# The up projection of the second batch as seven products of half blocks, with sums of blocks kept on chip

## The chip, the cores and the metric

The kernel runs on one core of one Trainium2 chip. The metric is device time in microseconds for one execution. Both request batches (1024 tokens each) go through the same layer within that one execution.

## What the kernel must compute

The reference is a hybrid encoder layer. What matters here is its feed-forward part, which each batch passes after the attention half:

```python
def _conv_ffn(x, l, prm):
    h = x @ prm['ffn_up'][l]                     # (1024, 1024) @ (1024, 5632)
    cw = prm['conv_w'][l]
    h = cw[0] * _shift_prev(h) + cw[1] * h + cw[2] * _shift_next(h) + prm['conv_b'][l]
    gate, up = jnp.split(h, 2, axis=-1)
    return (jax.nn.gelu(gate, approximate=False) * up) @ prm['ffn_down'][l]

x = _layer_norm(ALPHA * x + mixed, ...)
x = _layer_norm(ALPHA * x + _conv_ffn(x, l, prm), ...)
```

## The kernel before

All dense products are made in a split form: every float32 operand is written as a high part (`hi`, rounded to float32r by a ScalarE copy) and a low part (`lo`, the rest), and a product is three matmuls, hi·hi, hi·lo and lo·hi. The activations lie transposed in SBUF as `self.xT` = (`xh`, `xl`), each [128, 8 blocks of the model dimension, 1024 tokens]. Weights come from DRAM as 128 x 1024 blocks (`weights`, L229) or pairs of 128 x 512 (`load` in `dense_t`, L274), and are split by ScalarE (`hi`, L248) and GpSimd (`lo`, L251).

The feed-forward part has two stages for each batch. `phase_f1` (L1057) is the up projection. Its loop over j runs over 22 blocks of 128 gate columns; for each j it takes the gate block m = j and the up block m = 22 + j. Each m is one [128, 1024] tile of PSUM (`dpsum`, tag `d`, two buffers of two banks each) filled by `dense` (L253): two halves of 512 tokens, 8 blocks of the model dimension, three matmuls each, so 48 matmuls. Then ScalarE and VectorE do the width-3 convolution out of PSUM (L1070, L1071, L1073), GELU and the gating product (L1076, L1077), and the hidden block is split into hi and lo (`hilo`, L304). `phase_f2` (L1085) is the down projection, for four 128-token tiles at a time (j = 0, 1), over two halves of the output columns (n = 0, 1) and 22 blocks k.

The second batch's two stages are the last ones of the kernel, with nothing else left to interleave. There the hidden blocks of the first 512 tokens stay in SBUF (`keep`, 22 blocks of [128, 2, 512]); those of the other 512 tokens are stored to DRAM as they are made and loaded back during the second stage, into the space of `xh` and `xl`.

Two things order the work. The program is written with tiles and tags: tiles of one tag share a fixed number of buffers (`BUFS`: seven of `t`, four of `w`, two of `whi`; four PSUM banks for the two-buffer tag `d`, four for `spsum`'s tags `a` and `b`). And a planner lays out each engine's instruction order when the program is built, by priority (the order of the code) and by its own estimate of when each instruction is ready:

```python
with tile.TileContext(nc, schedule_with_timeline_sim=True) as tc, ExitStack() as ctx:
```

On the chip each engine runs its list in that order and waits on semaphores. All loads and stores named here are issued by SyncE (line 79, `ld`).

## Time and profile before

| | |
|---|---|
| median of 3 runs | 3606.48 us (3603.18 to 3615.9) |
| the profiled execution's own time | 3613.08 us |
| its span in the trace | 3611.3 us |
| mean granted TensorE clock | 0.944 |
| TensorE matmul busy | 3254.0 us, 90% of the span |
| up projection of the second batch, from the turn to full rate to its last matmul | about 2866 to 3345 us |
| down projection of the second batch and end | 3345 to 3611 us |

The lines of a trace give the kernel's line, the engine (PE is TensorE's matmuls, PEld its weight loads, DVE VectorE, ACT ScalarE, POOL GpSimd, SP SyncE; a q behind the name is the engine's queue), the operation, the tiles written and read, their shapes, and times in microseconds unless marked ns. A matmul's duration overlaps that of the next one, so the rate is read from a count over a stretch of time. PEclk is the granted clock of TensorE as a share of its full 2.4 GHz.

### The profile page before, as it was taken

How to read it: one execution, taken by the hardware profiler on the slowest of the kernel's cores; microseconds unless marked ns; L12 is line 12 of the kernel's file. 1: busy time of each engine (PE TensorE's matmuls, PEld its weight loads, DVE VectorE, ACT ScalarE, POOL GpSimd, SP SyncE). 2: the span in 40 equal slices, each digit the busy share in tenths (PEclk: the TensorE clock that was granted, in tenths of full speed). 3: DMA queues.
4: the chain of work that ended last, by engine and by line, in shares of the span. 5: the costliest groups of instructions: out<-in, count | busy, mean ns of one | idle time of the engine just before them, and what ended most of it. 6: DMA issues, size and time to landing. Idle time of an engine off the chain costs nothing. (4 is left out here: it accounts for less than half of the span.)

```text
span 3611.3 us, 56096 instructions
## 1 busy us (share of the span) xinstructions
PE 3254.0 (90%) x21477; PEld 2584.8 (72%) x21477; DVE 1961.5 (54%) x3550; ACT 1379.4 (38%) x2349; POOL 1292.2 (36%) x1387
## 2 busy tenths in 40 slices
PE   5788888998999986789999999989987899999997
PEld 4566666676777874567777787767865688888876
DVE  6378873335557866888534445366685633333022
ACT  3233332443245643345334343334454422332222
POOL 5365441001422445544121112363352622222464
PEclk9898888998999998788999999999999999999999
DMA  5568774534455655567543336586552322222642
GB/s 161 163 201 228 211 193 126 154 106 118 128 171 155 215 200 165 162 153 166 127 133 115 117 104 210 175 261 209 185 188 93 114 71 71 70 70 70 225 172 87
DMA packets 603360, 545.59 MB, mean 151 GB/s; under 512 B 205341, under 2 KB 477965, under 8 KB 603093
## 3 DMA queue, kind: packets, MB, share of 16 engines
q1 hardware_dynamic: 536532, 508.44, 46.3%
q10 hardware_dynamic: 66560, 33.56, 3.9%
q8 instruction: 171, 2.80, 0.3%
q14 instruction: 97, 0.79, 0.1%
HBM read 361.49 MB, written 180.39 MB: 150 GB/s over the span
## 5 line engine op out<-in xcount | busy, mean ns | idle before, releaser
L251 POOL TENSOR_TENSOR w<-w,whi 128x256 fp32r<-128x256 f32 (+1 forms) x800 | 758.6, 975 | 1246.1 <-ACT whi L248 1088.0
L264 PE MATMUL d<-xh,whi 128*128 128x512 f32 (+1 forms) x2112 | 863.7, 409 | 17.8 <-DVE t L399 6.0
L265 PE MATMUL d<-xl,whi 128*128 128x512 f32 (+1 forms) x2112 | 855.2, 405 | 0.6 <-DVE xl L308 0.6
L266 PE MATMUL d<-xh,w 128*128 128x512 f32 (+1 forms) x2112 | 853.7, 404 | 2.1 <-POOL w L251 2.1
L248 ACT ACTIVATE whi<-w 128x512 fp32r<-128x512 f32 (+1 forms) x536 | 307.9, 622 | 728.7 <-PE d L290 234.5
L264 PEld LDWEIGHTS d<-xh,whi 128*128 128x128 f32 (+1 forms) x2112 | 408.7, 194 | 117.3 <-issue 8.8
L266 PEld LDWEIGHTS d<-xh,w 128*128 128x128 f32 (+1 forms) x2112 | 407.9, 193 | 99.7 <-POOL w L251 3.3
L265 PEld LDWEIGHTS d<-xl,whi 128*128 128x128 f32 (+1 forms) x2112 | 408.2, 193 | 93.5 <-issue 2.0
L1071 DVE SCALAR_TENSOR_TENSOR t<-d,cols,t 128x1023 f32<-128x1023 f32 x88 | 112.8, 1282 | 455.7 <-ACT t L1070 442.6
L288 PE MATMUL d<-whi,xh 128*128 128x512 f32 x640 | 259.2, 413 | 31.5 <-DVE t L1051 15.1
L289 PE MATMUL d<-w,xh 128*128 128x512 f32 x640 | 259.2, 405 | 0.9 <-POOL w L251 0.9
L290 PE MATMUL d<-whi,xl 128*128 128x512 f32 x608 | 245.7, 404 | 0.0
L1051 DVE SCALAR_TENSOR_TENSOR t<-t,d 128x512 f32<-128x512 f32 x112 | 72.7, 678 | 244.7 <-PE d L290 240.7
L928 ACT ACTIVATE e<-e,ms 128x1024 f32<-128x1024 f32 x128 | 147.1, 1149 | 123.8 <-DVE ms L926 105.3
L935 POOL TENSOR_SCALAR e<-e,ms 128x512 f32<-128x512 f32 x128 | 88.1, 701 | 268.8 <-DVE ms L933 110.7
L288 PEld LDWEIGHTS d<-whi,xh 128*128 128x128 f32 x640 | 123.9, 194 | 66.7 <-DVE rs L1051 11.9
L739 DVE TENSOR_TENSOR G<-s,ms 64x256 f32<-64x256 f32 x128 | 53.4, 417 | 171.4 <-PE s L724 170.3
L289 PEld LDWEIGHTS d<-w,xh 128*128 128x128 f32 x640 | 124.0, 194 | 29.5 <-POOL w L251 2.2
L290 PEld LDWEIGHTS d<-whi,xl 128*128 128x128 f32 x608 | 117.2, 193 | 28.3 <-issue 1.0
L919 PE MATMUL s<-k,qh 128*128 128x512 f32 x256 | 113.9, 446 | 25.9 <-DVE ms L922 15.6
L619 DVE TENSOR_TENSOR Ntmp<-N 128x30 f32<-128x30 f32 (+14 forms) x240 | 111.3, 464 | 34.0 <-DMA N<-abd 29.0
L758 POOL COPY vr<-v 128x256 f32<-128x256 f32 x32 | 13.0, 405 | 324.4 <-DMA v<-va 311.3
(228 smaller groups left out, 5944.9 us busy)
## 6 DMA issues: line engine op xcount, KB each, us to landing
w<-in_ffn_up SPq DMA_DIRECT2D x88, 512.0 KB
w<-in_ffn_down SPq DMA_DIRECT2D x88, 512.0 KB
h<-t SPq DMA_DIRECT2D x66, 512.0 KB
ab<-AB ACTq DMA_DIRECT2D x64, 512.0 KB
w<-in_w_in SPq DMA_DIRECT2D x58, 512.0 KB
G<-ab SPq DMA_DIRECT2D x128, 128.0 KB
BK<-ab SPq DMA_DIRECT2D x64, 256.0 KB
w<-in_w_out SPq DMA_DIRECT2D x32, 512.0 KB
```

The costliest lines, as they stand in the source:

```text
L248: nc.scalar.activation(out=hi[:, s], in_=w[:, s], func=AF.Copy)
L251: nc.gpsimd.tensor_tensor(out=lo[:, s], in0=w[:, s], in1=hi[:, s].bitcast(F32), op=ALU.subtract)
L264: nc.tensor.matmul(o, wh, rh, start=first, stop=False)
L265: nc.tensor.matmul(o, wh, rl, start=False, stop=False)
L266: nc.tensor.matmul(o, wl, rh, start=False, stop=last)
L288: nc.tensor.matmul(out[i], lh, wh, start=k == ks[0], stop=False)
L289: nc.tensor.matmul(out[i], lh, wl, start=False, stop=False)
L290: nc.tensor.matmul(out[i], ll, wh, start=False, stop=k == ks[-1])
L619: nc.vector.tensor_tensor(out=tv, in0=N[:, 0:j, j : j + 1].to_broadcast([P, j, w]), in1=N[:, j : j + 1, j + 1 : 32].to_broadcast([P, j, w] ...
L919: nc.tensor.matmul(pp, q_[0], k_[c][:, ks], start=True, stop=False)
L928: nc.scalar.activation(out=e_, in_=e_, func=AF.Exp, bias=ms[:, 2 + c : 3 + c], accum_out=ms[:, 4 + c : 5 + c])
L1071: nc.vector.scalar_tensor_tensor(out=o[:, 1:T], in0=pp[:, 0 : T - 1], scalar=self.cw[0][:, m : m + 1], in1=o[:, 1:T], op0=ALU.mult, op1=AL ...
```

## The change

In the second batch, and there only, the up projection for j = 2 to 21 is no longer made by `dense`. The pair of weight blocks (gate and up, 256 columns by 1024) and the activations (1024 by 1024 tokens) are each seen as 2 x 2 blocks, and their product is made by seven half-block products (12 matmuls each) in place of eight, by the scheme of Winograd: sums S1 to S4 of weight blocks are formed for each j by VectorE and split anew; sums T1 to T4 of activation blocks are formed once, at j = 2, by `right`, of which T1, T2 and T4 have tiles of their own and T3 is written over the activation block b12 in `xh` and `xl`. Partial sums that enter more than one result are passed on inside PSUM by ScalarE copies between matmul groups, and one product (`e`) is added by VectorE. The space of `keep` is now taken by T, S and the split sums (`o`), so all hidden blocks go to DRAM, and the down projection loads all of them back, into the space of the seven right-hand blocks (28 slots, in the order in which `seven` uses them). `pre` is now called in both halves n; in the attention output stage it does nothing for n = 1. The first batch keeps its path.

```diff
-    def phase_f1(self, b, keep=None):
+    def phase_f1(self, b, tl=None):
...
         for j in range(KF):
             gu = []
-            for m in (j, KF + j):
-                ws = self.weights(I["ffn_up"][0], m * P, KT)
-                pp = self.dpsum()
-                self.dense(pp, ws, rhs, (0, 1), KT)
+            if tl and j == 2:
+                right = self.right(tl)
+            pps = self.seven(tl, j, right) if tl and j >= 2 else None
+            for i, m in enumerate((j, KF + j)):
+                pp = pps[i] if pps else eight(m)
...
             for half in range(2):
-                stay = keep is not None and half == 0
-                o = keep[:, j] if stay else self.dt("t", F32R, shape=(P, 2, 512))
+                o = self.dt("t", F32R, shape=(P, 2, 512))
                 self.hilo(gu[1][:, 512 * half : 512 * half + 512], o[:, 0], o[:, 1])
-                if not stay:
-                    self.ld(out=S["h"][j][half], in_=o)
...
+                self.ld(out=S["h"][j][half], in_=o)
+        return right[:7] if tl else None
+
+    def right(self, tl):
+        nc = self.nc
+        xh, xl = self.xT
+        block = lambda a, b: [tuple(x[:, 4 * a + k, 512 * b : 512 * b + 512] for x in (xh, xl)) for k in range(4)]
+        T = [tl(f"T{i}", dt=F32R, shape=(P, 4, 2, 512)) for i in (1, 2, 4)]
+        op = lambda out, a, b, o: nc.vector.tensor_tensor(out=out, in0=a, in1=b, op=o)
+        two = lambda: self.dt("t", shape=(P, 2, 512))
+        for q in range(2):
+            b11, b12, b21, b22 = ([x[:, 4 * a + 2 * q : 4 * a + 2 * q + 2, 512 * b : 512 * b + 512].bitcast(F32)
+                                   for x in (xh, xl)] for a in range(2) for b in range(2))
+            at = [t[:, 2 * q : 2 * q + 2] for t in T]
+            t1, u = two(), two()
+            op(t1, b12[0], b11[0], ALU.subtract)
+            nc.gpsimd.tensor_tensor(out=u, in0=b12[1], in1=b11[1], op=ALU.subtract)
+            op(t1, t1, u, ALU.add)
+            self.hilo(t1, at[0][:, :, 0], at[0][:, :, 1])
+            op(t1, b22[0], t1, ALU.subtract)
+            op(t1, t1, b22[1], ALU.add)
+            self.hilo(t1, at[1][:, :, 0], at[1][:, :, 1])
+            op(t1, b21[0], t1, ALU.subtract)
+            op(t1, t1, b21[1], ALU.add)
+            self.hilo(t1, at[2][:, :, 0], at[2][:, :, 1])
+            t3, u = two(), two()
+            op(t3, b22[0], b12[0], ALU.subtract)
+            nc.gpsimd.tensor_tensor(out=u, in0=b22[1], in1=b12[1], op=ALU.subtract)
+            op(t3, t3, u, ALU.add)
+            self.hilo(t3, *(x[:, 2 * q : 2 * q + 2, 512:1024] for x in (xh, xl)))
+        of = lambda t: [(t[:, k, 0], t[:, k, 1]) for k in range(4)]
+        return [of(T[0]), block(0, 0), of(T[1]), block(1, 0), block(0, 1), block(1, 1), of(T[2])]
+
+    def seven(self, tl, j, right):
+        nc, w = self.nc, self.I["ffn_up"][0]
+        raw = []
+        for m in (j, KF + j):
+            raw.append(self.dt("w", shape=(P, 8, P)))
+            self.ld(out=raw[-1], in_=w[:, m * P : (m + 1) * P].rearrange("(k p) c -> p k c", p=P))
+        a11, a12, a21, a22 = (r[:, 4 * h : 4 * h + 4] for r in raw for h in range(2))
+        op = lambda out, a, b, o: nc.vector.tensor_tensor(out=out, in0=a, in1=b, op=o)
+        s1, s2, s3, s4 = (tl("S", 4, shape=(P, 4, P)) for _ in range(4))
+        op(s1, a21, a22, ALU.add)
+        op(s2, s1, a11, ALU.subtract)
+        op(s4, a12, s2, ALU.subtract)
+        op(s3, a11, a21, ALU.subtract)
+        ha, la = self.dt("whi", F32R, shape=(P, 8, P)), self.dt("w", F32R, shape=(P, 8, P))
+        left = {}
+        for name, a in (("s1", s1), ("a11", a11), ("s2", s2), ("a12", a12), ("s3", s3), ("s4", s4), ("a22", a22)):
+            if name in ("a11", "a12"):
+                hi, lo = (x[:, 0:4] if name == "a11" else x[:, 4:8] for x in (ha, la))
+            else:
+                hi, lo = (tl("o", 16, F32R, (P, 4, P)) for _ in range(2))
+            nc.scalar.activation(out=hi, in_=a, func=AF.Copy)
+            nc.gpsimd.tensor_tensor(out=lo, in0=a, in1=hi.bitcast(F32), op=ALU.subtract)
+            left[name] = hi, lo
+
+        def product(o, a, b, first):
+            (ah, al), b = left[a], right[b]
+            for k in range(4):
+                for x, (l, r) in enumerate(((ah, 0), (ah, 1), (al, 0))):
+                    nc.tensor.matmul(o, l[:, k], b[k][r], start=first and k == x == 0, stop=k == 3 and x == 2,
+                                     skip_group_check=True)
+
+        e, p1, p2 = self.spsum(), self.dpsum(), self.dpsum()
+        c11, c12, c21, c22 = (p[:, 512 * h : 512 * h + 512] for p in (p1, p2) for h in range(2))
+        product(e, "s1", 0, True)
+        product(c11, "a11", 1, True)
+        nc.scalar.copy(out=c12, in_=c11)
+        product(c12, "s2", 2, False)
+        nc.scalar.copy(out=c21, in_=c12)
+        product(c11, "a12", 3, False)
+        product(c21, "s3", 4, False)
+        es = self.dt("t")[:, 0:512]
+        nc.scalar.copy(out=es, in_=e)
+        op(c22, c21, es, ALU.add)
+        product(c12, "s4", 5, False)
+        op(c12, c12, es, ALU.add)
+        product(c21, "a22", 6, False)
+        return p1, p2
...
-    def phase_f2(self, b, out, keep=None):
+    def phase_f2(self, b, out, slots=None):
...
-                parts = [(range(KF), {k: keep[:, k] if j == 0 else slots[k] if k < 16 else keep[:, k - 16] for k in range(KF)})]
+                at = {(jj, k): slots[(KF * jj + k) % len(slots)] for jj in range(2) for k in range(KF)}
+                parts = [(range(KF), {k: at[j, k] for k in range(KF)})]
+
+            def fill(jj, k):
+                for x in range(2):
+                    self.ld(out=at[jj, k][x], in_=S["h"][k][jj][:, x])
...
-                    if keep is None or j == 1 and k >= 16:
-                        self.ld(out=at[k], in_=S["h"][k][j])
-                    elif j == 0 and 4 <= k < 20:
-                        self.ld(out=slots[k - 4], in_=S["h"][k - 4][1])
+                    if slots is None:
+                        if n == 0:
+                            self.ld(out=here[k], in_=S["h"][k][j])
+                    elif j == 0 and n == 0:
+                        for kk in range(4) if k == 0 else ():
+                            fill(0, kk)
+                        if k + 4 < KF:
+                            fill(0, k + 4)
+                    elif j == 0:
+                        fill(1, k)
...
         with self.tc.tile_pool(name="f1", bufs=1) as pool:
-            h = pool.tile([P, KF, 2, 512], F32R, name="h")
-            self.phase_f1(1, h)
-            self.phase_f2(1, y1, h)
+            def tl(tag, bufs=1, dt=F32, shape=(P, 512)):
+                return pool.tile(list(shape), dt, name=self.nm(tag), tag=tag, bufs=bufs)
+
+            right = self.phase_f1(1, tl)
+            self.phase_f2(1, y1, [at for block in right for at in block])
```

## Rows read from the trace of the kernel before

**Rows 1.** the page, busy time of each engine over the span

```profile
PE 3254.0 (90%) x21477; PEld 2584.8 (72%) x21477; DVE 1961.5 (54%) x3550; ACT 1379.4 (38%) x2349; POOL 1292.2 (36%) x1387
```

**Rows 2.** stages: length, busy us (instructions) by engine, PEclk, DMA share, GB/s

```profile
2905.00:3000.00 95.00, 95.00 (x409) 76.96 (x408) 30.78 (x29) 29.04 (x39) 24.14 (x35) 1.00 0.23 75
...
3345.00:3365.00 20.00, 19.16 (x83) 15.19 (x82) 5.08 (x5) 5.71 (x9) 7.59 (x6) 1.00 0.95 361
3365.00:3465.00 100.00, 99.89 (x441) 82.36 (x440) 3.68 (x6) 21.91 (x38) 48.09 (x38) 1.00 0.45 154
```

**Rows 3.** groups of 2905 to 3345 us: shapes xcount, busy us, mean ns, idle

```profile
L264 PE MATMUL d<-xh,whi 128*128 128x512 f32 x629 | 249.9, 397 | 0.0
...
L251 POOL TENSOR_TENSOR w<-w,whi 128x256 fp32r<-128x256 f32 x152 | 108.0, 742 | 317.6 <-ACT whi L248 317.6
...
L1071 DVE SCALAR_TENSOR_TENSOR t<-d,cols,t 128x1023 f32<-128x1023 f32 x39 | 50.0, 1283 | 270.3 <-ACT t L1070 270.3
L1070 ACT ACTIVATE t<-d,cols 128x1024 f32<-128x1024 f32 x39 | 46.5, 1192 | 0.0
L248 ACT ACTIVATE whi<-w 128x512 fp32r<-128x512 f32 x78 | 45.0, 624 | 175.3 <-PE d L265 92.8 <-issue 77.0 <-PE d L266 5.4
L1077 DVE TENSOR_TENSOR t<-t,t 128x1024 f32<-128x1024 f32 x19 | 23.3, 1226 | 0.7
L1076 ACT ACTIVATE t<-t 128x1024 f32<-128x1024 f32 x20 | 21.2, 1062 | 54.6 <-DVE t L1073 54.6
L308 DVE TENSOR_TENSOR t<-t,t 128x512 fp32r<-128x512 f32 x20 | 13.7, 685 | 0.0
...
L307 ACT ACTIVATE h<-t 128x512 fp32r<-128x512 f32 x19 | 12.0, 632 | 74.7 <-DVE t L1077 74.7
```

**Rows 4.** duration ns min/median/max of single lines

```profile
L1051 DVE SCALAR_TENSOR_TENSOR t<-t,d x24: 670/681/689, 2794.1 to 3594.4; 128x512 f32<-128x512 f32 x24
...
L307 ACT ACTIVATE xh<-s x16: 572/582/600, 2813.5 to 2860.0; 128x512 fp32r<-128x512 f32 x16
```

**Rows 5.** the group of L251 at 512 columns, 3365 to 3590 us

```profile
L251 POOL TENSOR_TENSOR w<-w,whi 128x512 fp32r<-128x512 f32 x80 | 101.5, 1290 | 102.3 <-ACT whi L248 102.3
```

**Rows 6.** SyncE in order of time, one load pair of the first stage

```profile
2998.05 11.57 SPq L79 DMA_DIRECT2D w<-in_ffn_up  x2
```

**Rows 7.** SyncE's waits, 2860 to 3600 us: total, times, longest

```profile
SPq L79 <- PE d L266: 297.7, 46, 11.5
```

**Rows 8.** SyncE in order of time at the second stage's start

```profile
3345.25 0.38 SPq L79 DMA_DIRECT2D w<-in_ffn_down  x1
3345.68 0.94 SPq L79 DMA_DIRECT2D xh<-h  x2
3346.67 2.77 SPq L79 DMA_DIRECT2D t<-x  x4
```

**Rows 9.** the turn between the stages in order of time

```profile
3345.02 0.40 PE L288 MATMUL d<-whi,h 128*128 128x512 f32 x1
...
3348.64 1.28 DVE L1073 SCALAR_TENSOR_TENSOR t<-d,cols,t 128x1023 f32<-128x1023 f32 x1
...
3349.81 0.39 PE L288 MATMUL d<-whi,h 128*128 128x512 f32 x1
...
3351.75 0.62 ACT L307 ACTIVATE t<-t 128x512 fp32r<-128x512 f32 x1
```

**Rows 10.** the turn into the first stage, in 20 us windows

```profile
2820.00:2840.00 20.00, 17.10 (x82) 12.82 (x81) 19.25 (x33) 8.26 (x14) 14.77 (x13) 1.00 0.38 131
2840.00:2860.00 20.00, 15.35 (x76) 11.67 (x74) 15.56 (x21) 9.12 (x16) 16.88 (x16) 0.91 0.36 132
2860.00:2880.00 20.00, 19.37 (x72) 15.51 (x73) 4.07 (x5) 7.41 (x9) 5.72 (x8) 0.84 0.19 53
```

**Rows 11.** TensorE in order of time after the gap

```profile
2865.06 0.63 PE L264 MATMUL d<-xh,whi 128*128 128x512 f32 x1
```

**Rows 12.** line L334 on VectorE, beside GpSimd's half: ns min/median/max

```profile
L334 DVE TENSOR_TENSOR t<-t,t x44: 675/1205/1865, 8.5 to 3604.7; 128x512 f32<-128x512 f32 x44
```

More of the change, by code (lines that the diff above doesn't have):

```diff
@@ L1053, in residual @@
         for n in range(2):
-            self.dense_t(w, 512 * n, ks, lhs, range(4 * g, 4 * g + 4), put, n, pre if n == 0 else None, last and n == 1)
-    def phase_f1(self, b, keep=None):
+            self.dense_t(w, 512 * n, ks, lhs, range(4 * g, 4 * g + 4), put, n, lambda k: pre(k, n), last and n == 1)
+    def phase_f1(self, b, tl=None):
         nc, I, S = self.nc, self.I, self.st[b]
@@ L1086, in phase_f2 @@
+    def phase_f2(self, b, out, slots=None):
         nc, I, S = self.nc, self.I, self.st[b]
         gb = []
-        slots = [x[:, k0 + k].rearrange("p (a t) -> p a t", a=2) for k0 in (0, 4) for x in self.xT for k in range(4)]
+        own = [x[:, k0 + k].rearrange("p (a t) -> p a t", a=2) for k0 in (0, 4) for x in self.xT for k in range(4)]
         for j in range(2):
@@ L1091, in phase_f2 @@
             rs = {}
[L1092 to L1093 removed]
+            if slots is None:
+                parts = [(range(k0, min(k0 + 8, KF)), {k: own[8 * ((3 * j + k0 // 8) % 2) + k % 8] for k in range(k0, min(k0 + 8, KF))})
                          for k0 in range(0, KF, 8)]
             else:
[L1096 removed]
```

23 lines of the change are left out of this document (15 added, 8 removed).

## The prediction

> **What bounds the kernel now.** I read the page first: TensorE is busy for 3254.0 us, VectorE for 1961.5, ScalarE and GpSimd for less than 1400 each [rows 1]. A whole-kernel share proves nothing for one stage, so the second view is the one by windows. In the up projection of the second batch TensorE is busy 95.00 us of 95.00 at a granted clock of 1.00, while VectorE, ScalarE and GpSimd stand at 24 to 31 us of those 95 [rows 2]. The third view, by line, gives the rate: the groups of L264, L265 and L266 have 629 matmuls each in the 440 us from 2905 to 3345, with no idle time in front of them [rows 3], so one matmul takes 440 / 1887 = 0.2332 us. This stage is TensorE throughput and nothing else; work taken off TensorE here is worth its full price as long as no wait appears in its place. The down projection behind it is the same: 99.89 us busy of 100 [rows 2]. The chain that ended last runs through these matmuls in both stages, so I costed the change on TensorE's list and asked of every other engine only whether TensorE will wait for it.
>
> **What is removed.** A pair of blocks cost 2 x 48 = 96 matmuls and costs 7 x 12 = 84 now. For 20 pairs that is 240 matmuls fewer: 240 x 0.2332 = **56.0 us**, the ceiling of the gain. One new pair is 84 x 0.2332 = 19.6 us of TensorE.
>
> **What is added on other engines, per pair.** VectorE: four convolution passes of 1.283, the gating product 1.226, two low parts of 0.685 [rows 3], the four sums S at the nearest price, that of a low part (0.685), two additions out of PSUM at 0.68, the row of L1051 [rows 4]: 5.13 + 1.23 + 1.37 + 2.74 + 1.36 = 11.8 us. ScalarE: two convolution passes 1.192, GELU 1.062, two high parts 0.632, seven splits 0.624 [rows 3], three copies out of PSUM at 0.582, the row that reads PSUM [rows 4]: 10.8 us. GpSimd: seven subtractions at 1.290 [rows 5] = 9.0 us. All are below 19.6, so none becomes the bound by throughput. The weights have a lead: 16 buffers of `o` hold a pair and a half, so they are split about a pair ahead. These additions cost nothing while that cover lasts.
>
> **Waits that are new, per pair.** Before, a PSUM tile had a whole block's time (48 x 0.2332 = 11.2 us) to be emptied. Now two waits stand on TensorE's list. First, a11 must be copied from c11 to c12 before s2 adds to it: no other product of the pair is free then (a12 adds to c11, which is being copied). That is one copy, 0.582, plus the drain of the last matmul (its 0.397 duration less the 0.233 rate [rows 3]) and whatever ScalarE has in hand: I take 1.0 to 1.3 us. The second copy (c12 to c21) lies under a12, 2.8 us. Second, p1 is final only after s4 and the addition of e, and must be read out before the next pair's a11: 0.68 + 1.192 + 2 x 1.283 = 4.4 us [rows 3, 4], of which a22 covers 12 x 0.2332 = 2.8. The rest, 1.6 plus queueing behind one operation in flight, about 2.3, can be covered by the next pair's s1, which goes into `e` and needs neither p1 nor p2. p2 has three further products as cover and costs nothing. The planner does fill such gaps with later products: at the turn into the down projection TensorE goes on without a break from 3345.02 to 3349.81 while the second PSUM tile is still being read by L1073 [rows 9]. But one s1 (2.8 us) has to fill two gaps that sum to 3.3 to 3.6. Bounds: 0.2 us per pair if the filling works out, 2.9 if each gap stays open once. I take 0.9, close to the filled case because of [rows 9]: 20 x 0.9 = **18 us**.
>
> **The sums of activations, once.** `right` has 24 VectorE passes over 1024 columns at 1.226 [rows 3], 29.4 us, and eight high parts and four GpSimd subtractions beside them. Whether TensorE waits depends on when they may start. Their inputs are ready before the stage begins, and VectorE is two thirds idle there. But they need `t` buffers, and buffers of a tag seem to be given in the order of the code. The load of the next weight block waits for the last matmul that reads a low part (297.7 us in 46 waits) [rows 6, 7], although a raw block's buffer was free much earlier, when GpSimd finished its split; that free one is held for the low part that precedes the load in the code. Likewise the four `t` loads of the down projection, coded ahead of the two `xh` loads, are issued behind them [rows 8]. By that order the sums start when the pair j = 1 gives its last `t` tile, 6.7 us after its last matmul (3345.02 to 3351.75 for the last pair [rows 9]), and VectorE ends them 29.4 us later at the earliest. a22 for T4 stands at the end: 6.7 + 29.4 + half of a22, 1.4, = 37.5 us from j = 1 to the end of j = 2, where 19.6 are due: 18 us lost, less 2.8 if s1 of j = 3 fills in. The gap also lowers the clock: ahead of this stage TensorE was busy for 15.35 of 20 us, and in the next 20 us the granted clock averaged 0.84, a matmul showing 0.63 us in place of 0.40 [rows 10, 11], which is 0.16 x 20 = 3 us. Bounds: 2 (sums done early, only T3's split, which must wait for j = 1's reads, in the way; a12 and three other products cover it) and 21. I take **15**.
>
> **The turn and the down projection.** At the end no s1 is left as cover, so p1's and p2's read-out shows: 2 us (0 to 5). The hidden blocks of the first 512 tokens now come from DRAM: 768 KB per block k in 2.8 us is 281 GB/s. Before, 16 of the 22 blocks had the same load (other halves fetched ahead), at 361 GB/s with TensorE busy 19.16 of 20 us [rows 2]. The slots come free in the order of the last pair's products, from its s1 on, some 17 us before they are read. SyncE's queue has more, shorter issues (0.47 us each [rows 8]): 61 in 61 us, half its time. I take 2 us (0 to 8). For the stores, doubled, the DMA engines have room at 75 GB/s [rows 2]. The attention output stage and the first batch issue the same instructions as before.
>
> **Sum.** -56.0 + 18 + 15 + 2 + 2 = **-19 us**. From the profiled execution's 3613.08 that is 3594; it stood 6.6 above the median of the runs shown, so against 3606.48 I predict **3587.5 us**. Its own range: 3576 to 3599.
>
> **The rivals.** (1) *The sums start early*: buffers are given as they come free and `right` runs under j = 0 and 1. The idle VectorE speaks for it, [rows 6 to 8] against. Entry 2 in place of 15: 3574.5, down to 3562 with 0.3 us per pair. (2) *The gaps stay open*: the copy and part of p1's read-out cost TensorE 1.85 us per pair; 20 x 1.85 = 37, with the 19 elsewhere, gives the whole gain back: 3606. For it: the plan is laid out from estimates, and a list that is off by 0.5 us in two places cannot be reordered. (3) *VectorE and GpSimd block each other, slower*: a VectorE sum of two SBUF tiles of 512 columns takes 0.685 in this stage [rows 3] but 1.205 at the median and 1.865 at most where GpSimd works at the same time [rows 12]. GpSimd will be busy 9 of 19.6 us beside S sums, low parts and the gating product. If each of the two entries of VectorE into p1's read-out finds such an operation in its way, the read-out is 4.4 + 2 x 1.2 to 1.9 = 6.8 to 8.2; less 5.6 of cover that leaves 1.2 to 2.6, and with the open copy gap 2.2 to 3.9 per pair. At 3.0: 60 + 19 - 56 = +23, 3629. It decides for slower from 1.85 us per pair on. Against it: the passes that matter read PSUM, and L1051, at work beside GpSimd, stays within 670 to 689 ns [rows 4]; only what stands ahead of them in the queue can be long. The Trainium skill, SBUF — State Buffer, section "Who interferes with whom", has this as a rule: a VectorE instruction with two SBUF inputs and a GpSimd instruction that reads SBUF hold each other up for their whole length, while one with at most one SBUF input is free of it; [rows 12] and [rows 4] agree, and by the rule the sum is that of rival 3 only if the planner puts such passes ahead of the read-out. That the change does not do what it says can't be: the 240 matmuls are a count of the code.
>
> **How the numbers follow.** Chances: the forecast 0.45, rival 1 0.17, rival 2 0.20, rival 3 0.18. A difference under 0.3% (10.8 us) can hardly be told from none here. 0.05 of the forecast's chance lies within it, so faster 0.57, same 0.25, slower 0.18. The range, 3562 to 3622, reaches to rival 1's low end and into rival 3, and leaves out the deeper part of each.
>
> **What would show it.** In the changed profile: 21,237 matmuls; GpSimd at 9 to 11 us per pair and VectorE at 12 to 15; an idle time of about 1 us before each s2 put down to ScalarE; s1 standing behind a22 of the pair before; a gap of some 10 to 15 us at j = 2 with VectorE busy, and a granted clock below 1 just after. It is wrong if the idle time in front of a11 put down to VectorE passes 2 us per pair, if the gap at j = 2 is missing, or if weights or hidden blocks land late in the down projection.

## The result, and the profile after

The changed kernel takes 3638.68 us at the median, beside 3609.53 for the kernel before. The ratio of their runs is 1.0089 (95% interval 1.0066 to 1.0112), so it is some 32 us slower (24 to 40; the two medians alone differ by 29). I had forecast 19 us less, and the range ended at 3622. The page of the changed kernel, its line of busy times, beside [rows 1]:

```profile
PE 3210.8 (88%) x21237; PEld 2538.3 (70%) x21237; DVE 2122.8 (58%) x3694; ACT 1458.3 (40%) x2477; POOL 1395.9 (38%) x1371
```

The 240 matmuls are gone and TensorE is busy 43 us less. So over 70 us were added as waiting. To place them I measure the stage itself, from its first matmul to the first L288 of the down projection. TensorE in order of time, first the kernel before (its L288 is in [rows 9]), then the changed one:

```profile
2860.63 1.22 PE L264 MATMUL d<-xh,whi 128*128 128x512 f32 x2 [0.69 <-ACT xh L307]
```

```profile
2864.73 1.22 PE L264 MATMUL d<-xh,whi 128*128 128x512 f32 x2 [0.69 <-ACT xh L307]
...
2920.96 1.22 PE L1157 MATMUL s<-T,o 128*128 128x512 f32 x2 [18.68 <-ACT T L307]
...
2928.71 4.99 PE L1157 MATMUL s<-T,o 128*128 128x512 f32 x12 [6.53 <-DVE T L308]
...
3116.32 3.00 PE L1157 MATMUL d<-T,o 128*128 128x512 f32 x12 [0.66 <-ACT d L1164]
3120.39 0.50 PE L1157 MATMUL d<-xh,whi 128*128 128x512 f32 x1 [1.06 <-ACT d L1166]
...
3370.82 0.47 PE L288 MATMUL d<-whi,T 128*128 128x512 f32 x1 [1.95 <-ACT t L1080]
```

The stage is 3345.02 - 2860.63 = 484.4 us before and 3370.82 - 2864.73 = 506.1 after, 21.7 longer. The GELU of one pair follows that of the last by 22.40 us before, in every pair past the entry, and by 21.48 after (median). By "entry" I mean the passage from eight products to seven, at j = 2, and by "turn" that into the down projection. That splits the stage: 240 matmuls fewer, -56.0; 20 pairs at 21.48 - 84 x 0.2333 = 1.88 above their matmuls, +37.6; the turn, +1.95; the rest, +38.2, is the entry. Behind the stage nothing changed: 3611.3 - 3345.02 = 266.3 us and 3637.3 - 3370.82 = 266.5. The stage and what follows thus account for 22 of the 32 us. Where the other 10 arise is not shown (under "Ahead of the stage" below).

**The pairs.** TensorE's groups of the changed kernel from 3000 to 3300 us, with the idle time ahead of each and what ended it:

```profile
L1157 PE MATMUL d<-T,o 128*128 128x512 f32 x336 | 82.4, 394 | 9.2 <-ACT d L1164 9.2
...
L1157 PE MATMUL d<-xh,whi 128*128 128x512 f32 x112 | 45.6, 407 | 15.0 <-ACT d L1166 15.0
```

s2 waits for the first ScalarE copy (L1164), and a12 for the second (L1166): 0.66 and 1.07 us in each of 14 pairs, and no other wait stands in these 300 us. I had costed one copy and the read-out of p1. TensorE where p1 is read out, with s1 (`s<-T,o`), a22 and the first matmul of the next pair's a11:

```profile
3107.27 2.68 PE L1157 MATMUL s<-T,o 128*128 128x512 f32 x11
3109.79 2.88 PE L1157 MATMUL d<-T,o 128*128 128x512 f32 x12
...
3112.74 0.40 PE L1157 MATMUL d<-xh,whi 128*128 128x512 f32 x1
```

p1's read-out costs nothing, since eleven matmuls of s1 stand ahead of a22 and cover it together with a22. For the same reason s1 covers neither copy. ScalarE in order of time around the second copy:

```profile
3118.22 1.15 ACT L307 ACTIVATE t<-t 128x512 fp32r<-128x512 f32 x2 [1.95 <-DVE t L1087]
3119.28 0.57 ACT L1170 COPY t<-s 128x512 f32<-128x512 f32 x1
3119.74 0.59 ACT L1166 COPY d<-d 128x512 f32<-128x512 f32 x1
```

The copy takes 0.59 us, but it stands behind two splits of the hidden block and the copy of `e`. s2 ends at 3119.32, so the copy starts 0.4 us late.

**The entry.** Windows of the changed kernel, the columns of [rows 2]:

```profile
2880.00:2905.00 25.00, 22.28 (x98) 17.94 (x96) 15.40 (x14) 11.99 (x18) 15.42 (x12) 1.00 0.35 113
2905.00:2930.00 25.00, 2.51 (x5) 1.60 (x6) 24.93 (x16) 5.37 (x9) 15.12 (x7) 0.51 0.18 63
2930.00:2960.00 30.00, 23.97 (x82) 17.52 (x82) 25.85 (x23) 12.55 (x17) 13.76 (x6) 0.84 0.06 18
...
3100.00:3200.00 100.00, 93.08 (x399) 74.03 (x398) 64.16 (x60) 47.18 (x68) 49.24 (x34) 1.00 0.29 100
```

VectorE is busy 24.93 of 25 us while TensorE does 2.51, at a granted clock of 0.51 (its lower level, 1.2 GHz). VectorE in order of time:

```profile
2902.77 0.69 DVE L1136 TENSOR_TENSOR S<-w 128x512 f32<-128x512 f32 x1 [6.42 <-DMA w<-in_ffn_up]
...
2907.60 1.27 DVE L1081 SCALAR_TENSOR_TENSOR t<-d,cols,t 128x1023 f32<-128x1023 f32 x1
...
2912.99 4.49 DVE L1101 TENSOR_TENSOR t<-xh 128x1024 f32<-128x1024 f32 x2
...
2920.88 3.37 DVE L1101 TENSOR_TENSOR t<-t,t 128x1024 f32<-128x1024 f32 x1
...
2955.33 1.23 DVE L308 TENSOR_TENSOR T<-t,T 128x1024 fp32r<-128x1024 f32 x1
```

VectorE stands 6.42 us on an S sum whose weights are late, with j = 1's convolution behind it, so `right` begins at 2912.99. Its 24 passes end at 2956.56, 43.6 us later, where I had 29.4: five take 2.2 to 3.4 us in place of 1.21, some 8.5 us in all, and S sums and a wait of 2.82 us lie between them. TensorE's waits for T sum to 30.0 us of the entry's 38.2. The granted clock of 0.84 in the 30 us behind the gap takes some 5 more (an estimate, 0.16 x 30).

### The profile page after: what moved, and what is told of

Same layout as the page of the kernel before. It is cut to its first block, busy times and chain, and to the rows that moved or that the text cites. A ratio compares the mean times of both kernels' runs of the same rounds, so it can differ in the third digit from the quotient of the medians.

```text
span 3637.3 us, 56288 instructions
## 1 busy us (share of the span) xinstructions
PE 3210.8 (88%) x21237; PEld 2538.3 (70%) x21237; DVE 2122.8 (58%) x3694; ACT 1458.3 (40%) x2477; POOL 1395.9 (38%) x1371
## 5 line engine op out<-in xcount | busy, mean ns | idle before, releaser
L251 POOL TENSOR_TENSOR w<-w,whi 128x256 fp32r<-128x256 f32 (+2 forms) x640 | 643.3, 1031 | 938.8 <-ACT whi L248 766.7
L264 PE MATMUL d<-xh,whi 128*128 128x512 f32 (+1 forms) x1472 | 608.0, 414 | 18.4 <-ACT whi L248 6.6
L266 PE MATMUL d<-xh,w 128*128 128x512 f32 x1472 | 597.0, 406 | 2.3 <-POOL w L251 2.3
L265 PE MATMUL d<-xl,whi 128*128 128x512 f32 x1472 | 597.7, 406 | 0.6 <-DVE xl L308 0.6
L248 ACT ACTIVATE whi<-w 128x512 fp32r<-128x512 f32 x456 | 261.7, 621 | 563.3 <-PE d L290 229.2
L264 PEld LDWEIGHTS d<-xh,whi 128*128 128x128 f32 (+1 forms) x1472 | 286.5, 195 | 89.2 <-issue 9.3
L288 PE MATMUL d<-whi,xh 128*128 128x512 f32 x768 | 308.5, 413 | 30.5 <-DVE t L1053 14.7
L266 PEld LDWEIGHTS d<-xh,w 128*128 128x128 f32 x1472 | 285.4, 194 | 70.6 <-POOL w L251 3.4
L265 PEld LDWEIGHTS d<-xl,whi 128*128 128x128 f32 x1472 | 286.5, 195 | 64.8 <-issue 2.0
L289 PE MATMUL d<-w,xh 128*128 128x512 f32 x768 | 311.4, 405 | 1.0 <-POOL w L251 1.0
L288 PEld LDWEIGHTS d<-whi,xh 128*128 128x128 f32 x768 | 148.8, 194 | 72.0 <-DVE t L1053 12.2
L1150 POOL TENSOR_TENSOR o<-S,o 128x512 fp32r<-128x512 f32 x80 | 116.0, 1452 | 188.5 <-ACT o L1149 130.4
```

The costliest lines, as they stand in the source:

```text
L248: nc.scalar.activation(out=hi[:, s], in_=w[:, s], func=AF.Copy)
L251: nc.gpsimd.tensor_tensor(out=lo[:, s], in0=w[:, s], in1=hi[:, s].bitcast(F32), op=ALU.subtract)
L264: nc.tensor.matmul(o, wh, rh, start=first, stop=False)
L265: nc.tensor.matmul(o, wh, rl, start=False, stop=False)
L266: nc.tensor.matmul(o, wl, rh, start=False, stop=last)
L288: nc.tensor.matmul(out[i], lh, wh, start=k == ks[0], stop=False)
```

## The experiments

All times are medians. Each kernel ran beside its own runs of the kernel before, whose medians lay between 3603.3 and 3609.5, so small differences between rows are better read from the ratio and the stage. "Pair" is the median distance of the GELUs; "entry" is worked out as above: stage - 484.4 + 2.8 for each pair with seven products - the pairs' excess over 19.60 - the turn's 1.95 where it shows. It doesn't hold the 2.8 us of each pair that keeps eight products: two more in e11 to e14 and e18, three in e16 and e17. It is blank where the pairs differ much among themselves. Line numbers are those of each kernel, and cuts in the code are marked by three dots.

| kernel | us | ratio to before (95%) | stage | pair | entry |
|---|---|---|---|---|---|
| changed | 3638.7 | 1.0089 (1.0066 to 1.0112) | 506.1 | 21.48 | 38 |
| e1 | 3632.7 | 1.0064 (1.0047 to 1.0080) | 503.5 | 21.76 | 30 |
| e2 | 3655.1 | one run | 513.2 | 21.76 | 40 |
| e3 | 3591.0 | 0.9962 (0.9944 to 0.9979) | 464.1 | 19.30 | 40 |
| e4 | 3732.5 | 1.0346 (1.0331 to 1.0362) | 597.0 | 27.6 | |
| e5 | 3621.6 | 1.0039 (1.0026 to 1.0053) | 487.1 | 21.48 | 19 |
| e6 | 3707.5 | 1.0280 (1.0263 to 1.0298) | 575.8 | 24.7 | |
| e7 | 3688.6 | 1.0231 (1.0212 to 1.0250) | 558.9 | 24.5 | |
| e8 | 3647.1 | 1.0108 (1.0089 to 1.0127) | 511.1 | 21.75 | 38 |
| e9 | 3609.7 | 1.0003 (0.9994 to 1.0013) | 476.6 | 21.02 | 20 |
| e10 | 3619.5 | 1.0036 (1.0023 to 1.0049) | 482.3 | 21.63 | 13 |
| e11 | 3622.3 | 1.0042 (1.0029 to 1.0054) | 489.5 | 21.48 | 20 |
| e12 | 3602.4 | 0.9987 (0.9976 to 0.9998) | 470.5 | 21.09 | 10 |
| e13 | 3613.1 | 1.0020 (1.0007 to 1.0032) | 481.4 | 21.06 | 21 |
| e14 | 3618.0 | 1.0035 (1.0023 to 1.0047) | 489.3 | 21.48 | 20 |
| e15 | 3652.7 | 1.0126 (1.0109 to 1.0143) | 520.2 | 21.76 | 47 |
| e16 | 3596.3 | 0.9982 (0.9971 to 0.9994) | 463.9 | 20.94 | 4 |
| e17 | 3577.9 | 0.9929 (0.9914 to 0.9944) | 444.5 | 19.72 | 6 |
| e18 | 3576.9 | 0.9924 (0.9903 to 0.9945) | 442.9 | 19.72 | 7 |

### The copies (e3, e4)

```diff
-        nc.scalar.copy(out=c12, in_=c11)
-        product(c12, "s2", 2, False)
-        nc.scalar.copy(out=c21, in_=c12)
+        product(c12, "s2", 2, True)
         product(c11, "a12", 3, False)
-        product(c21, "s3", 4, False)
+        product(c21, "s3", 4, True)
```

> Leaves out the two copies of partial sums inside PSUM (c11 to c12 and c12 to c21), so c12, c21 and c22 lack those terms; all products and additions stay. Theory (the two copies open the two gaps of each pair): the steady pair falls from 21.5 to 19.6 to 19.9 us and the time by 30 to 37 us against the changed kernel. Rival (the copies only show the wait, and weights, VectorE or the read-out of p1 set the pair's pace): another gap takes their place, the pair stays above 20.8 us and the time falls by less than 15.

e3 leaves out the two copies, and with them the partial sums that they carry on. Without them a pair takes 19.30 us, and the window 3100 to 3200 of e3 has no idle time on TensorE:

```profile
3100.00:3200.00 100.00, 100.00 (x438) 81.79 (x437) 75.44 (x67) 46.13 (x67) 54.75 (x38) 1.00 0.32 110
```

The stage is 42 us shorter than in the changed kernel with the entry as dear as ever. The theory held: the whole excess of the pairs belongs to the two copies.

```diff
-        nc.scalar.copy(out=c21, in_=c12)
         product(c11, "a12", 3, False)
+        nc.scalar.copy(out=c21, in_=c12)
```

> Only the order in the code: product a12 stands ahead of the copy c12 to c21. Theory A (the wait of a12 for that copy comes from the order of the code, since the two touch different banks of one PSUM tile and are tracked as one): a12 follows s2 at once, but the copy then waits for a12 and s3 for the copy; one gap of about 1 us moves and nothing is gained, within 6 us of the changed kernel. Theory B (tracked by region): a12 covers the copy, one of the two gaps goes, 0.8 to 1.1 us per pair, 16 to 22 us in all.

94 us slower than the changed kernel, which neither theory had. The copy now starts behind a12, 0.86 us or more after its last matmul in all 20 pairs, though a12 writes c11 and the copy reads c12. Both orders fit a wait for the tile p1 as a whole, as theory A has it. s1 moved to cover the copy, and p1's read-out lost its cover. TensorE's waits of e4, 2990 to 3450 us (total, times, longest):

```profile
PE d L1157 <- ACT d L1164: 38.4, 18, 6.0
PE d L1157 <- DVE t L1083: 35.8, 18, 2.0
```

That is the pair of waits I had forecast, each left open, at 27.6 us a pair: 8.0 above the matmuls, where I had bounded both at 2.9. The two waits make 4.1 of it. Over 3100 to 3200 us of e4 the granted clock is 0.90 in the mean, which the bound did not have.

### The sums of activations where they stood (e1, e2, e5, e8)

e1 takes the temporaries from the ring `o`, in pieces of 512 columns, so that they need no `t` buffer; e2 has the same pieces in `t`. e5 is e1 with GpSimd's part done by VectorE; e8 is the changed kernel with that edit alone.

```diff
-        two = lambda: self.dt("t", shape=(P, 2, 512))
-        for q in range(2):
+        two = lambda: tl("o", 16, F32, (P, 512))    # e1, e5; e2: self.dt("t", shape=(P, 512))
+        for q in range(4):
...
-            nc.gpsimd.tensor_tensor(out=u, in0=b12[1], in1=b11[1], op=ALU.subtract)
-            op(t1, t1, u, ALU.add)
+            op(t1, t1, b12[1], ALU.add)                 # e5, e8
+            op(t1, t1, b11[1], ALU.subtract)
...                                                       # t3 likewise
```

> The temporaries of the activation sums come from the ring o, which is unused before j = 2, in pieces of 512 columns; what is computed and where it stands in the code are as in the changed kernel. Theory (the sums start late because they wait for t buffers behind j = 1): they run under j = 0 and 1, the gap at j = 2 shrinks from 41 us to under 8, and the time falls by 33 to 38 us against the changed kernel, to about 3603. Rival (the 29 us of VectorE passes, stretched by GpSimd, are the bound wherever they stand): the gap stays above 20 us and the time falls by less than 15, to 3624 or more.

> Control for the first kernel: the same pieces of 512 columns, but still in buffers of t. Theory: the start stays as late as in the changed kernel (about 2910 us), the gap at j = 2 stays at 35 to 45 us and the time within 6 us of the changed kernel's. Rival (the smaller pieces, not the buffers, open the gap): the time falls as in the first kernel.

> As the first kernel (sums in ring o, pieces of 512 columns), and the low parts are subtracted by VectorE in place of GpSimd, 56 passes in place of 48. In the first kernel 13 of the passes stood ahead of j = 0's convolution on VectorE, took 1.2 to 1.6 us each in place of 0.69, and TensorE waited 14.3 us for that convolution. Theory (the stretch by GpSimd makes the pieces hold up the convolution): the passes come back to 0.69, the wait falls below 4 us, and the time falls by 10 us or more against the first kernel, to 3622 or less. Rival (the passes delay the convolution by their count alone, since VectorE takes them as soon as they are ready): within 6 us of the first kernel's 3633.

> The changed kernel with one edit: the four low-part subtractions of the activation sums are made by VectorE in place of GpSimd (28 passes of 1024 columns in place of 24), t buffers kept. In the changed kernel the passes span 43.6 us in place of 29.4, several taking 2.2 to 3.4 us. Theory (GpSimd's own four subtractions stretch them): the span falls below 38 us although there are four more, and the time falls by 4 to 10 us. Rival (the stretch comes from other work in VectorE's queue and from waits): the span grows by about 5 and the time by 3 to 6.

e1 gained 6 us, 2.6 in the stage, and its interval overlaps that of the changed kernel: the time is the rival's. But the sums did start early, 0.6 us after the stage's first matmul. In e2, with the same pieces in `t`, they start 47.1 us after it, in the changed kernel 48.3, so the `t` buffers were what held them. The planner set 13 passes ahead of j = 0's convolution, and TensorE waited 14.3 us for L1083. The first eight of them:

```profile
2863.16 12.72 DVE L1101 TENSOR_TENSOR o<-xh 128x512 f32<-128x512 f32 x8
```

e5 gained 11 more and left 7.9 us of that wait: the entry halves, 38 to 19. Eight such passes without GpSimd's subtractions take 4.89 us (shown for e11 below). e8, where the sums still wait for `t`, gained nothing, and e2's stage, from one run, is 7.1 us longer than that of the changed kernel. In e8 the stretch did go: 28 passes span 39.4 us in place of 43.6 for 24. But the planner laid passes of several T side by side, ScalarE's split of the first T starts 58.8 us after the stage's first matmul in place of 55.1, TensorE's first wait for T grew from 18.7 to 21.5 us, and the entry stayed at 38. So a shorter span is worth nothing here unless the pass that TensorE waits for comes earlier.

In e1, e2, e8 and e15 the pair is 21.75 or 21.76, not 21.48: there two matmuls of s1 stand ahead of a12, cover the second copy, and wait 1.3 us themselves for ScalarE's split of S.

### s1 divided over the gaps (e6, e7, e9, e10)

```diff
-        product(e, "s1", 0, True)
-        product(c11, "a11", 1, True)
+        product(e, "s1", 0, True, slice(0, 4), getattr(self, "s3", None))   # behind s3 of the pair before
+        last = product(c11, "a11", 1, True)
         nc.scalar.copy(out=c12, in_=c11)
-        product(c12, "s2", 2, False)
+        product(e, "s1", 0, True, slice(4, 8), last)
+        last = product(c12, "s2", 2, False)
         nc.scalar.copy(out=c21, in_=c12)
-        product(c11, "a12", 3, False)
-        product(c21, "s3", 4, False)
+        product(e, "s1", 0, True, slice(8, 12), last)
...
+        product(c12, "s4", 5, False)
+        product(c11, "a12", 3, False)
+        op(c12, c12, es, ALU.add)
+        self.s3 = product(c21, "s3", 4, False)
         op(c22, c21, es, ALU.add)
-        product(c12, "s4", 5, False)
-        op(c12, c12, es, ALU.add)
         product(c21, "a22", 6, False)
```

The edit does two things: it divides s1, and it puts s4 and a12 ahead of s3. The addition into c22, which needs s3 and is needed by a22, then has four matmuls of s1 as its only cover.

> Only the order of the products of a pair: a11, a third of s1, s2, a third of s1, s4, a12, s3, a third of the next pair's s1, a22; c12 gets e after a12. Theory (each pair loses its 2.3 us to three short waits, for the two copies and for the addition into c22, because one undivided s1 can stand in one place only, and p1's read-out is covered by s3 and a22): the pair falls from 21.5 to 19.3 to 19.9 us and the time by 30 to 44 us against the changed kernel, to 3595 to 3609. Rival (planner's estimates and ScalarE's queue, in which a copy stands behind other work, open gaps longer than a third of s1): the pair stays above 20.8 and the time falls by less than 14.

> The two together: sums in ring o without GpSimd, and the new order of products. If the entry and the pair lose time independently, the gains add up: about 16 from the entry and 37 from the pairs, 3585, below the kernel before. If the entry's loss only moves elsewhere once the pairs run faster (weights landing late, VectorE's queue), it stays within 6 us of the one with the new order alone.

The copy gaps all but closed (2.5 us in 7 waits of e7, 2990 to 3410 us), and the pair still rose to 24.7 and 24.5: a22 now waited for the c22 addition, 55.4 us in 16 waits of that stretch. For e6 that is the rival's time, though by another wait than the rival's. VectorE and then TensorE of e7 in order of time:

```profile
3161.48 1.73 DVE L1136 TENSOR_TENSOR S<-w 128x512 f32<-128x512 f32 x1 [6.66 <-DMA w<-in_ffn_up]
3163.14 0.69 DVE L1136 TENSOR_TENSOR d<-d,t 128x512 f32<-128x512 f32 x1
3163.74 1.18 DVE L1136 TENSOR_TENSOR S<-S,w 128x512 f32<-128x512 f32 x1
3165.03 1.57 DVE L1136 TENSOR_TENSOR S<-w,S 128x512 f32<-128x512 f32 x1
3166.52 1.74 DVE L1136 TENSOR_TENSOR S<-w,w 128x512 f32<-128x512 f32 x1
3168.19 0.69 DVE L1136 TENSOR_TENSOR d<-d,t 128x512 f32<-128x512 f32 x1
...
3168.93 5.14 PE L1158 MATMUL d<-T,o 128*128 128x512 f32 x12 [4.40 <-DVE d L1136]
...
3202.19 2.89 PE L1158 MATMUL d<-T,o 128*128 128x512 f32 x12
```

A sum S that waits 6.66 us for weights stands on VectorE, three more sums follow, and the 0.69-us addition for which TensorE waits is behind them. The twelve matmuls after the wait take 5.14 us; twelve without one take 2.89. A window of e7:

```profile
3100.00:3200.00 100.00, 83.90 (x326) 65.57 (x325) 54.07 (x51) 39.54 (x59) 38.49 (x28) 0.90 0.26 84
```

The granted clock is 0.90 in the mean. Why the weights are late was not tested. In these 100 us the queue of SyncE, which issues the loads, waits 45.8 us for low parts of hidden blocks (L308) and 44.1 us for S sums.

```diff
-        op(s1, a21, a22, ALU.add)
...                                                       # s2, s4, s3 likewise
+        pool = lambda out, a, b, o: nc.gpsimd.tensor_tensor(out=out, in0=a, in1=b, op=o)      # e9
...
+        pool(s1, a21, a22, ALU.add)                                                           # e9
...
+        with self.tc.issue_after(self.c22.ins) if hasattr(self, "c22") else nullcontext():    # e10
+            op(s1, a21, a22, ALU.add)                     # behind the c22 addition of the pair before
```

> The kernel of e7 (s1 split over the two copy gaps and the gap before a22, own ring, no GpSimd work in the sums of activations), with the four sums S of each pair moved from VectorE to GpSimd, so that no operation that waits for a late weight load stands on VectorE. Theory (in e7 TensorE waits 4.4 us before a22 because the c22 addition stands on VectorE behind an S sum that waits 6.7 us for its weight load, and behind the other S sums): the wait before a22 falls below 1 us, a pair takes 19.5 to 20.5 us in place of 25, and the time is 3590 to 3610. Rival (what holds the c22 addition is the convolution of the previous tile, or GpSimd at about 15 us a pair becomes late with the splits): the pair stays above 21.5 us and the time above 3625.

> The kernel of e7 with the four sums S kept on VectorE, but issued only behind the c22 addition of the pair before. Theory (the same as for e9): the wait before a22 goes, since only convolution passes can stand ahead of the c22 addition; but S sums that wait for weights now stand ahead of the convolution of the pair's first tile, so that a11 of the next pair may wait 1 to 2 us. 20 to 22 us a pair, 3600 to 3640. Rival (the late weight loads only move the wait from a22 to a11, in full): no gain over e7, 3670 or more.

79 and 69 us less than e7, by nothing but the place of four sums. That settles that the sums ahead of the addition made the wait of e7. e9's pair, 21.02, is above what I expected: a22 still waited 0.4 and s4, for the second copy, 0.7 us. In e10 a22 still waits 26.9 us in 20 waits, and the pair of 21.63 lies where I expected it.

### The sums of activations spread (e11 to e16)

e11 gives a quarter of the sums out behind each of j = 0 to 3 and begins the seven products at j = 4; e12 is e11 with e9's edits.

```diff
-            if tl and j == 2:
+            if tl and j == 4:
...
+            if tl and j < 4:
+                self.part(tl, j)        # quarter j of the sums; T3 is split at j = 4
```

> The kernel of e5 (own ring, no GpSimd work in the sums) with the sums of activations given out in four quarters behind the gating products of j = 0 to 3, and the seven products from j = 4 on (18 pairs in place of 20); T3 is kept unsplit until j = 4. The matmuls of two pairs, 24 x 0.228 = 5.5 us, come back. Theory (the entry is dear because the sums stand on VectorE in a block ahead of convolution passes for which TensorE waits): with 14 us of idle VectorE time per pair the quarter of some 9 us fits, the entry loss falls from about 34 us in e5 to under 12 with the 5.5 in it, and the time is 3592 to 3603. Rival (the planner puts the passes ahead of the convolution again, or the late weights and not the sums hold VectorE up): TensorE still waits for L1083, and the time stays within 8 us of e5's 3621.6.

> The sums spread as in e11 together with the product order and GpSimd sums of e9. If both theories hold, 216 matmuls fewer (49 us), some 5 us at the entry, 18 x 0.3 to 1 us at the gaps and 4 us at the end: 3565 to 3585, below both kernels. If the gaps stay open the time is e9's less the entry, above 3595.

The rival held for e11. Its VectorE, then its TensorE, in order of time:

```profile
2864.94 4.89 DVE L1102 TENSOR_TENSOR o<-xh 128x512 f32<-128x512 f32 x8
2869.76 6.71 DVE L1102 TENSOR_TENSOR o<-o,xl 128x512 f32<-128x512 f32 x11
2876.38 1.28 DVE L1081 SCALAR_TENSOR_TENSOR t<-d,cols,t 128x1023 f32<-128x1023 f32 x1
2877.57 5.26 DVE L1102 TENSOR_TENSOR o<-o,xl 128x512 f32<-128x512 f32 x5
...
2885.99 0.77 PE L264 MATMUL d<-xh,whi 128*128 128x512 f32 x1 [8.93 <-DVE t L1083]
```

The order of the code did not keep later quarters back; 19 passes ran ahead of j = 0's convolution. e12 came out by its second case, above 3595: the pairs are those of e9, 21.09, and the entry fell to 10. e13 and e14 hold each quarter behind its gating product, in e12 and e11:

```diff
+            gate = nc.vector.tensor_tensor(out=gu[1], in0=gu[0], in1=gu[1], op=ALU.mult)
...
-                self.part(tl, j)
+                with self.tc.issue_after(gate.ins):
+                    self.part(tl, j)
```

> The kernel of e12 with each quarter of the sums of activations issued only behind the gating product of its j (0 to 3). In e12 the planner put the passes of more than one quarter back to back ahead of a convolution pass, and TensorE waited 8.3 us for L1083 at about 2885, with a granted clock of 0.74 to 0.83 around it. Theory (the order of VectorE's list, not the amount of its work, makes the entry dear): that wait and the slow matmuls around it go, 10 to 14 us less than e12's 3602.4, 3588 to 3593, below the kernel before. Rival (the passes only move behind and hold up the next convolution or the splits for j = 4): less than 4 us gained, above 3598.

> The kernel of e11 (product order of the change, S sums on VectorE) with the same hold: the entry by itself. Theory: the 8.9-us wait for L1083 goes, 10 to 14 us less than e11's 3622.3, 3608 to 3612, with the pairs at 21.3 to 21.6 us as before. Rival: above 3618.

Both came out by the rival, e14 at its edge and e13 11 us above e12. The waits of 8 to 9 us for L1083 went, and another came: 16.6 us for a split of T at j = 4 in e13. The last quarter, behind j = 3's gating product, has no matmuls left to lie under. That was a fault of the experiment; e16 begins the seven products at j = 5.

> The kernel of e13 with the seven products from j = 5 on (17 pairs). In e13 TensorE waited 16.6 us at j = 4 for a split of T, because the last quarter of the sums, held behind the gating product of j = 3, can't begin before j = 3's last matmul. Now j = 4's 96 matmuls (22 us) cover it. One pair fewer costs 12 x 0.228 = 2.7 us. Theory (with the passes in order and under matmuls the entry costs nothing but the pairs that keep eight products): the waits of 16.6 + 3.4 us and the slow clock behind them (0.67 and 0.87 in the two 20-us windows) go, 20 to 28 us less than e13's 3613.1 with the pair's cost already in it: 3585 to 3593. Rival (VectorE's work, not its order, makes the entry dear; another wait takes its place): above 3602.

The entry fell from 21 to 4 us with the same passes on the same engine, and one more pair keeps its eight products (2.8 us). The time is 3 us above what I expected, as the pair stayed at 20.94. So the order of the passes and the matmuls over them set its price.

e15 is the changed kernel with e9's sums on GpSimd alone:

> The changed kernel with one edit: the four sums S of each pair on GpSimd in place of VectorE. In the changed kernel VectorE stood 6.4 us on an S sum that waited for its weight load, ahead of j = 1's convolution, and 2.2 us per pair on such waits later. Theory (in the changed order of products TensorE's gaps belong to the ScalarE copies, which no S sum delays by much, and VectorE's waits matter at the entry alone): the entry is up to 6 us shorter, the pair stays at 21.2 to 21.6 us, 3630 to 3637. Rival (late S sums on VectorE hold up the low parts L308, with them ScalarE's list and the copies): the pair falls below 20.8 us and the time below 3625. Third case (GpSimd, which does part of the sums of activations there, becomes late): no gain or slower, above 3639.

The third case, by its time. At the entry GpSimd is late: its first subtraction for T begins 50.4 us after the stage's first matmul in place of 44.9, behind four S sums, and the entry is 9 us dearer. The pairs make the rest, and there GpSimd is not the cause. TensorE waits for ScalarE's splits of S, 27.9 us in 18 waits, but it does so in e1 and e8 too (29.1 and 24.2 us, 18 waits each), where VectorE makes the sums. The edit that gave 79 us in e7 costs 14 here.

### The c22 addition first (e17, e18)

```diff
-                nc.vector.scalar_tensor_tensor(out=o[:, 1:T], in0=pp[:, 0 : T - 1], scalar=self.cw[0][:, m : m + 1],
...
+                with self.tc.issue_after(self.c22.ins) if pps else nullcontext():
+                    nc.vector.scalar_tensor_tensor(out=o[:, 1:T], in0=pp[:, 0 : T - 1], scalar=self.cw[0][:, m : m + 1],
...
```

> The kernel of e16 with the first convolution pass of each pair's first tile held behind the c22 addition. In e12 the planner put that pass (1.28 us) ahead of the addition, and a22 waited 0.35 to 0.70 us for it. Theory: that wait goes, 17 x 0.4 to 0.7 = 7 to 12 us less than e16. Rival (p1's read-out, now later by one addition, or the second copy's gap grows by as much): within 4 us of e16.

VectorE in order of time, e16 and then e17:

```profile
3139.79 1.28 DVE L1081 SCALAR_TENSOR_TENSOR t<-d,cols,t 128x1023 f32<-128x1023 f32 x1 [1.29 <-ACT t L1080]
3140.99 0.69 DVE L1147 TENSOR_TENSOR d<-d,t 128x512 f32<-128x512 f32 x1
```

```profile
3131.50 0.70 DVE L1148 TENSOR_TENSOR d<-d,t 128x512 f32<-128x512 f32 x1 [1.98 <-PE d L1171]
3132.11 1.28 DVE L1082 SCALAR_TENSOR_TENSOR t<-d,cols,t 128x1023 f32<-128x1023 f32 x1
```

One 1.28-us pass was held behind one 0.70-us addition, and the time fell by 18 us, more than expected: the waits for the second copy (6.9 us in 10 of e16, 2990 to 3300 us) went with those for the addition (7.1 us in 15). The planner laid out ScalarE's list anew as well. The second copy (L1181 in e16, L1182 in e17) stood behind two splits of the hidden block and now stands ahead of them:

```profile
3129.72 1.15 ACT L307 ACTIVATE t<-t 128x512 fp32r<-128x512 f32 x2 [2.41 <-DVE t L1087]
...
3131.30 0.58 ACT L1181 COPY d<-d 128x512 f32<-128x512 f32 x1
```

```profile
3122.31 0.58 ACT L1182 COPY d<-d 128x512 f32<-128x512 f32 x1
3122.82 1.14 ACT L307 ACTIVATE t<-t 128x512 fp32r<-128x512 f32 x2
```

How much of the 18 us belongs to each of the two changes in order I did not take apart. The same 100 us of e16 and of e17:

```profile
3100.00:3200.00 100.00, 95.24 (x403) 74.52 (x404) 44.81 (x42) 47.49 (x71) 67.22 (x53) 1.00 0.31 105
```

```profile
3100.00:3200.00 100.00, 99.62 (x427) 78.81 (x427) 50.57 (x47) 49.36 (x75) 72.21 (x57) 1.00 0.34 109
```

e18 gives each quarter out one j earlier, the first ahead of j = 0's convolution, and begins at j = 4.

> The kernel of e17 with every quarter of the sums given out one j earlier (the first ahead of j = 0's convolution, where VectorE stands idle for 10 us in the kernel before; the others behind the gating products of j = 0 to 2) and the seven products from j = 4 on: 18 pairs in place of 17. Theory: VectorE's idle time ahead of j = 0's convolution holds a quarter's 8 to 10 us, so that nothing waits, and the twelve matmuls saved show: 2.8 us less than e17's 3577.9, about 3575. Rival (the first quarter holds up j = 0's convolution, as in e11): TensorE waits for L1084's or L1086's pass at about 2885, 4 to 10 us more than e17.

TensorE did not wait for j = 0's convolution, but the stage is only 1.6 us shorter, and the medians can't be told apart. e17 and e18 are below both kernels, by 0.7% of the kernel before.

## Why the prediction was wrong, step by step

- **What is removed, -56.0:** right. 96 matmuls per 22.40 us is 0.2333 each, and e17 keeps most of it: 17 x 2.8 = 47.6 us removed, 39.9 off the stage.
- **The pairs, 18 forecast, 37.6 measured.** The step that failed is "one s1 (2.8 us) has to fill two gaps ... I take 0.9, close to the filled case because of [rows 9]". The planner put eleven of s1's twelve matmuls into one place, p1's read-out, and that wait vanished; both copies stayed open, at 0.66 and 1.07 us. "The second copy lies under a12" was false: a12 waits for it in every pair. The bounds, 0.2 and 2.9, did not follow from the working either: gaps of 3.3 to 3.6 less one s1 of 2.8 are 0.5 to 0.8, and open they are 3.3 to 3.6. Rival 2's mechanism, gaps left open in a fixed list, was the true one, though with the second copy in place of p1's read-out. That its price, 1.85 per pair, came within 0.03 of the measured one is luck: 1.85 was the price at which the gain is gone.
- **The entry, 15 forecast, 38.2 measured.** The failed step is "VectorE ends them 29.4 us later at the earliest", taken as the likely case. The sums start 13.9 us after j = 1's last matmul (2899.14) in place of 6.7, behind an S sum and its late weights (6.42), and the 24 passes took 43.6 us, 14.2 more. These make some 21 of the 23 missing. That `t` buffers hold the start back was right (e1, with e2 as control). That an earlier start would cost 2 us, rival 1, was wrong as the planner orders it (e1, e5, e11: 19 to 30) and nearly right with the order forced (e16: 4, beside three pairs that keep eight products).
- **VectorE and GpSimd (rival 3).** L1101's pass at 2920.88 took 3.37 us beside a GpSimd subtraction at 2919.90 to 2923.17, where others took 1.21. The Trainium skill, SBUF — State Buffer, section "Who interferes with whom", has a VectorE instruction with two SBUF inputs contend with a GpSimd instruction that reads SBUF, and calls the port pair that they share "an exclusive lock". The trace agrees: the pass ends 1.08 us after the subtraction does, about what it takes alone. It acted at the entry; in the changed kernel's pairs TensorE waited for VectorE once (2.0 us). In e7 the rival's place did come up: three S sums ahead of a PSUM addition took 4.45 us beside GpSimd's splits, where 3 x 0.69 would be 2.1. So some 2.4 of that 4.40-us wait may be the rival's stretch (an estimate), and the rest the order behind the late weights. e9 and e10 took both away at once and do not tell them apart.
- **Turn 2, down projection 2:** 1.95 and 0.2. Weights and hidden blocks were in time there; the weights of S were not.
- **Ahead of the stage, 0 forecast.** The span of the changed kernel's stage and what follows is 21.9 us longer, the ratio says 32. In e17 it is 38.8 shorter, the ratio says 25.6. By the same reckoning 4 to 13 us are missing in every kernel with a ratio here. TensorE's list is the same up to the stage. In the two traces the stage begins 4.1 us apart, but over all twenty its start varies from 2857.05 (e3) to 2873.67 us (e2), so single traces can't place 10 us there. This rests on one trace of before, whose execution stood 6.6 above the median that I predicted from, and on the assumption that its stage is as long in other executions; where the 10 us arise, and why, stays open.
- **The signs that I had named.** "It is wrong if" listed VectorE ahead of a11, a missing gap at j = 2, and late loads in the down projection. None of them came up; the wait ahead of a12 and the late weights for the S sums were not on the list. Of the signs that were to bear it out, s1 stood ahead of a22 of the pair before, not behind it, and the gap at j = 2 was 18.68 us long with more behind it, not 10 to 15.

Together: 19.6 + 23.2 - 1.8 + 10 = 51 us, from -19 to +32. The first three are read from the stage and what follows; the 10 is what the ratio leaves over.

## What to carry to other kernels

Where a list per engine is fixed ahead of time, cost a short operation for which the busy engine waits with everything that can stand ahead of it in its queue, and above all with what waits there for a transfer: in e7 a 0.69-us addition cost TensorE up to 4.4 us a pair, and moving four sums won 79. Count the fillers and the gaps one by one, ask which gap the planner will give each filler to, and look whether two halves of one tile are waited for as one. Work that is "off the path" because its engine is idle is free only if its order is forced behind what the busy engine needs, and if some matmuls are left to cover its last piece.

## What the runs showed of the hardware that was not expected

The price of a wait is more than the wait: in e7, with TensorE idle ahead of a22 for 55.4 us in 16 waits, the longest 4.4, the granted clock over 100 us was 0.90, and after such a wait twelve matmuls took 5.14 us in place of 2.89. With gaps of 0.66 and 1.07 us in each pair of the changed kernel it was 1.00. And 84 matmuls without idle time took 19.30 us in e3, 0.230 each, where the kernel before took 0.2333 at the same granted clock of 1.00; why was not looked into.
